# One decoder layer with PEER experts on one core: evacuation of the U products, order of the start and places of the last chunks changed

## The chip, the cores and the metric

The kernel runs on one NeuronCore of a Trainium2 chip. The metric is the device time of one execution in microseconds (us). Engines: PE (TensorE), ACT (ScalarE), DVE (VectorE), POOL (GpSimd), SP (SyncE, which issues DMAs here). One kernel launch computes the whole layer.

## The reference

For one sequence of 256 tokens with D = 2048 (T = 256 below) and one layer:

```
h = x + hybrid_mixer(rmsnorm(x, attn_norm), ...)          # NSA heads + sliding-window heads, out-projection
xn = rmsnorm(h, ffn_norm)
q = xn @ wq                                              # 8 heads, 2 halves of 128
s1, s2 = q[..., 0, :] @ subkeys[0].T, q[..., 1, :] @ subkeys[1].T
v1, i1 = top_k(s1, 16); v2, i2 = top_k(s2, 16)
sc, ci = top_k(v1[..., :, None] + v2[..., None, :], 16)  # 16 of the 256 sums
idx = i1[ci // 16] * 128 + i2[ci % 16]; gate = softmax(sc)
h = h + sum_k gate_k * gelu(xn . u[idx_k]) * v[idx_k]    # 16384 experts, U and V 16384 x 2048
out = rmsnorm(h, final_norm)
```

All of it is float32.

## The kernel before, in words

Matrix products that need float32 accuracy are made of three products of rounded parts: a matrix is split into a high part (`hi`, a rounded copy made by ACT, L114) and the rest (`lo`, raw minus hi, made by DVE, L115), and hi*Xhi + hi*Xlo + lo*Xhi are added in PSUM. `split` (L103) does that for the units of weights, which `load` (L93) brings in order through SP's queue; a unit is a [128, 1024] piece, 512 KB. `take` (L120) hands a unit to PE.

**Start.** `x` arrives in 8 pieces; `x_parts` (L153) makes its two halves (ACT L155, DVE L156). The V products (L244 to L246) run while `x` arrives; the squares of `x` (L249, ACT) are added by DVE (L258) and a matmul with ones sums them over partitions (L322, in `scale_rows`). `rms_scale` (L140) then makes the row of scales `rB` by ACT's square root (L146) and DVE's L147 to L151. The k and v projections (L173 to L175, `cols`) run meanwhile; the transposes of `rB` (L331), the gates (L340) and the compressed-key products (L304) stand among them in PE's order. Small tables (`posk`, `ohr`, `w2k` and so on) are issued on SP's queue as the code reaches them.

**Attention and out-projection** run to about 330 us, then the query projection of the PEER layer (`cols_wide`, L159) for 16 query columns i. Each i ends with `qs`: ACT copies one half of the product out of PSUM (L710), DVE adds the other (L711), PE multiplies with the sub-keys (L684), ACT scales into `ssb` (L687), and DVE takes the 16 best (`top16`, L672 to L678). Before the U products start, the scaled `x` is split once more into the two halves of X (ACT L717; L718 on DVE for even and POOL for odd blocks).

**U products.** 128 blocks of 128 experts. A block needs two units of U and either 16 pairs of a 512-column and a 256-column matmul (`cols_wide`: L165, L166; "wide") or 48 matmuls of 256 columns (`cols`: L173 to L175; "narrow", all three parts summed in one half of a PSUM bank). `u_end` (L656) empties the block's PSUM one block later: narrow by one Gelu of ACT (L662); wide by ACT's copy (L660), DVE's add (L661) and the Gelu. `product()` gives the next block one of a few PSUM buffers, so the block's first matmul (L165) waits until the older one is empty. The first `4 * LEAD` = 52 blocks run beside the routing:

```
            for n in range(4 * LEAD):
                u_block(n // 4, n % 4, n >= NARROW)
                settle()
                u_end(1)
                owed += BUDGET[n >= NARROW]
                while steps and owed > 0:
                    c, fn = steps.pop(0)
                    owed -= c
                    settle(1)
                    fn()
```

`steps` are the routing's pieces with estimated costs (candidate sums, top 16, picks by a one-hot comparison at L771 to L778 on DVE and POOL, index splits, `flip` with PE's transposes L793 to L795, `tok`), `BUDGET` how much of them is written per narrow and wide block. What is written is then ordered by a scheduler for each engine; `tc.high_priority()` moves a step ahead. Blocks 52 to 127 run beside the building of expert lists.

**V products and end.** 103 chunks of gathered V rows and weights, split like the rest (L1174, L1175; `a_parts`, `v_parts`), three products each (`v_products`, L1205) for two token halves t and four column quarters c. `finish` (L1233) adds a sum to the residual (L1236), squares it (L1238); `last_norm` (L1249) makes the scale r, scales (L1256, L1258) and issues the output DMAs (L1259).

Of the kernel before, what the change touches and what calls it, by code (L numbers as in the profile page):

```python
# [10 lines left out]
F32 = mybir.dt.float32  # L11
# [8 lines left out]
D = 2048  # L20
# [23 lines left out]
TG = 16  # L44
GSCALE = 2.0 ** 15
# [3 lines left out]
NARROW = 12  # L49
BUDGET = (2.75, 2.1)  # L50
# [4 lines left out]
def decoder_trunk(ctx, tc, xT, g1, g2, gf, w_cols, w_v, w_out, w_q, u, v, subk, posk, posv,  # L55
# [37 lines left out]
    def load():  # L93
# [6 lines left out]
        sp.dma_start(raw[:, :r * w], src)  # L100
        raws[i] = raw

    def split():  # L103
# [9 lines left out]
        with tc.high_priority():  # L113
            act.activation(hi[:, :n], raw[:, :n], AF.Copy)  # L114
            dve.tensor_tensor(lo[:, :n], raw[:, :n], f(hi[:, :n]), op=OP.subtract)  # L115
# [24 lines left out]
    def rms_scale(pool_, ps, dst):  # L140
# [5 lines left out]
        act.activation(s, ps, AF.Sqrt, bias=epst, scale=1.0 / D)  # L146
# [4 lines left out]
        dve.scalar_tensor_tensor(dst, s, 1.5, r, op0=OP.add, op1=OP.mult)  # L151

    def x_parts(db, src, g):  # L153

        act.activation(X[:, db, 0:T], src, AF.Copy, scale=g[:, db:db + 1])  # L155
        dve.scalar_tensor_tensor(X[:, db, T:], src, g[:, db:db + 1], f(X[:, db, 0:T]),  # L156
                                 op0=OP.mult, op1=OP.subtract)

# [27 lines left out]
    with ExitStack() as mx:  # L186
# [19 lines left out]
        sp.dma_start(g1t, g1)  # L206
# [26 lines left out]
        for k in range(8):  # L233
            if k + RAW < 8:
                load_x(k + RAW)
            for i in range(2):
                x_parts(2 * k + i, xt[:, 2 * k + i, :], g1t)
# [12 lines left out]
        sp.dma_start(relt[0:32, :], rel)  # L250
        sp.dma_start(ohrt, ohr)
        sp.dma_start(ohrbt, ohrb)
        sp.dma_start(pkv["k"], posk)
        sp.dma_start(pkv["v"], posv)
# [4 lines left out]
        sp.dma_start(g2t, g2)  # L259
        sp.dma_start(subkt, subk)  # L260
        sp.dma_start(w2kt, w2k)
        sp.dma_start(w2vt, w2v)
        sp.dma_start(sinkt, bass.AP(tensor=sinks.tensor, offset=sinks.offset, ap=[[0, 128], [1, 16]]))
# [47 lines left out]
        def tables():  # L311
            sp.dma_start(w1t["v"], w1v)
# [7 lines left out]
        def scale_rows():  # L320
            pss = ps1.tile([128, T], F32, name="tp", bufs=2)
            pe.matmul(pss, ones, ssum[:, 0], start=True, stop=True)  # L322
            sp.dma_start(w1t["k"], w1k)
# [270 lines left out]

        dve.tensor_scalar(nsink, sinkt, -1.0, None, op0=OP.mult)
# [36 lines left out]
    with ExitStack() as p3:  # L632
# [23 lines left out]
        def u_end(keep=0):  # L656
            while len(HU) > keep:
                ps, h, wide = HU.pop(0)
                if wide:
                    act.activation(h, ps[:, 1], AF.Copy)  # L660
                    dve.tensor_tensor(h, ps[:, 0], h, op=OP.add)  # L661
                act.activation(h, h if wide else ps[:, 0], AF.Gelu_apprx_tanh)  # L662

        with ExitStack() as pr:
# [34 lines left out]
            for i in range(1, 16):  # L699
# [10 lines left out]
                act.activation(qs, ps[:, 1], AF.Copy)  # L710
                dve.tensor_tensor(qs, ps[:, 0], qs, op=OP.add)  # L711
# [3 lines left out]
            with tc.high_priority():  # L715
# [707 lines left out]
```

## Time and profile before

| what | us |
|---|---|
| median of 3 runs (lowest, highest) | 1613.42 (1611.53, 1614.13) |
| the profiled execution | 1614.29 |
| its span, first to last instruction | 1612.5 |
| PE busy in it | 1586.9 (98%) |
| DVE busy | 1232.0 (76%) |
| ACT busy | 951.1 (59%) |
| POOL busy | 376.4 (23%) |

The profiled execution is 0.87 us above the median, and 1.8 us of it lie outside the span. PE's busy share says how little it idles, not that each of its matmuls runs at full speed: the granted clock in the windows says that. A wait names the instruction that released the waiting one.

### The profile page before, as it was taken

How to read it: one execution, taken by the hardware profiler on the slowest of the kernel's cores; microseconds unless marked ns; L12 is line 12 of the kernel's file. 1: busy time of each engine (PE TensorE's matmuls, PEld its weight loads, DVE VectorE, ACT ScalarE, POOL GpSimd, SP SyncE). 2: the span in 40 equal slices, each digit the busy share in tenths (PEclk: the TensorE clock that was granted, in tenths of full speed). 3: DMA queues.
4: the chain of work that ended last, by engine and by line, in shares of the span. 5: the costliest groups of instructions: out<-in, count | busy, mean ns of one | idle time of the engine just before them, and what ended most of it. 6: DMA issues, size and time to landing. Idle time of an engine off the chain costs nothing.

```text
span 1612.5 us, 26938 instructions
## 1 busy us (share of the span) xinstructions
PE 1586.9 (98%) x9870; PEld 1370.9 (85%) x9870; DVE 1232.0 (76%) x2291; ACT 951.1 (59%) x1638; POOL 376.4 (23%) x354
## 2 busy tenths in 40 slices
PE   9999999999999999999999999999999999999996
PEld 8998888888898888888888888888887878788885
DVE  7698886779999987678668767665555788888886
ACT  6587775554643666667545444444445676777675
POOL 0010111143133410000000000000003666677770
PEclk9999999999999999999999999999999999999998
DMA  9544434555455576666999976688765879899992
GB/s 318 172 156 128 135 121 146 182 175 178 158 173 167 160 252 218 216 207 238 299 334 356 307 247 206 209 265 276 234 221 210 317 280 340 297 365 346 347 348 81
DMA packets 135224, 378.33 MB, mean 235 GB/s; under 512 B 11976, under 2 KB 67372, under 8 KB 119212
## 3 DMA queue, kind: packets, MB, share of 16 engines
q1 hardware_dynamic: 115596, 257.51, 48.6%
q0 software_dynamic: 18912, 117.98, 19.5%
q8 instruction: 79, 1.29, 0.3%
q10 hardware_dynamic: 576, 1.05, 0.2%
q14 instruction: 61, 0.50, 0.1%
HBM read 341.05 MB, written 35.44 MB: 233 GB/s over the span
## 4 chain that ended last, share of the span: by engine, by line
PE 91%; DVE 5%; ACT 1%; issue 1%; POOL 1%; DMA 1%; SPq 0%; DVEq 0%; POOLq 0%; ACTq 0%
PE mm L165 29%; PE mm L166 15%; PE pv L1210 6%; PE pv L1212 6%; PE pv L1211 6%; PE mm L573 3%; PE mm L173 3%; PE mm L175 3%; PE mm L174 3%; PE mm L1210 2%; PE mm L1212 2%; PE mm L1211 2%; PE tp L837 2%; PE mm L574 2%; DVE lo L115 1%
## 5 line engine op out<-in xcount | busy, mean ns | idle before, releaser
L165 PE MATMUL mm<-X,hi 128*128 128x512 f32 x2096 | 751.7, 399 | 6.0 <-DVE hg L661 6.0
L114 ACT ACTIVATE hi<-raw 128x1024 fp32r<-128x1024 f32 (+1 forms) x370 | 389.8, 1055 | 401.1 <-issue 185.3
L115 DVE TENSOR_TENSOR lo<-raw,hi 128x1024 fp32r<-128x1024 f32 (+1 forms) x370 | 458.8, 1242 | 205.4 <-ACT hi L114 202.7
L166 PE MATMUL mm<-X,lo 128*128 128x256 f32 x2096 | 592.0, 283 | 0.4 <-DVE lo L115 0.4
L165 PEld LDWEIGHTS mm<-X,hi 128*128 128x128 f32 x2096 | 394.8, 188 | 97.8 <-DVE hg L661 6.9
L166 PEld LDWEIGHTS mm<-X,lo 128*128 128x128 f32 x2096 | 394.7, 188 | 1.7 <-DVE lo L115 1.4
L1175 DVE TENSOR_TENSOR lo<-hg,hi 128x1024 fp32r<-128x1024 f32 x210 | 256.1, 1224 | 68.8 <-ACT hi L1174 64.0
L1174 ACT ACTIVATE hi<-hg 128x1024 fp32r<-128x1024 f32 x210 | 221.6, 1058 | 95.7 <-PE pv L1212 76.9
L1084 POOL DMA_INDIRECT hg<-in_v_dram,idxV x103 | 129.3, 1256 | 451.4 <-ACT hg L662 296.8
L173 PE MATMUL mm<-X,hi 128*128 128x256 f32 x544 | 157.8, 290 | 0.0
L175 PE MATMUL mm<-X,lo 128*128 128x256 f32 x544 | 154.0, 283 | 0.2 <-DVE lo L115 0.2
L174 PE MATMUL mm<-X,hi 128*128 128x256 f32 x544 | 153.9, 283 | 0.0
L1092 POOL DMA_INDIRECT ar<-At,idxA x103 | 116.7, 1133 | 96.7 <-issue 60.4
L1211 PE MATMUL pv<-lo,ah 128*128 128x512 f32 x396 | 136.7, 395 | 0.0
L1212 PE MATMUL pv<-hi,al 128*128 128x512 f32 x396 | 135.3, 396 | 0.0
L1210 PE MATMUL pv<-hi,ah 128*128 128x512 f32 x396 | 123.0, 397 | 1.8 <-ACT ah L1162 1.6
L173 PEld LDWEIGHTS mm<-X,hi 128*128 128x128 f32 x544 | 103.7, 191 | 4.3 <-issue 3.9
L175 PEld LDWEIGHTS mm<-X,lo 128*128 128x128 f32 x544 | 103.3, 190 | 1.4 <-DVE lo L115 1.1
L174 PEld LDWEIGHTS mm<-X,hi 128*128 128x128 f32 x544 | 103.4, 190 | 0.5 <-issue 0.4
L1210 PEld LDWEIGHTS pv<-hi,ah 128*128 128x128 f32 x396 | 74.4, 188 | 21.8 <-ACT ah L1162 2.3
L1212 PEld LDWEIGHTS pv<-hi,al 128*128 128x128 f32 x396 | 74.4, 188 | 18.2
L1211 PEld LDWEIGHTS pv<-lo,ah 128*128 128x128 f32 x396 | 74.4, 188 | 17.5
(299 smaller groups left out, 2109.8 us busy)
## 6 DMA issues: line engine op xcount, KB each, us to landing
raw<-in_u_dram SPq DMA_DIRECT2D x256, 512.0 KB, 4.7
raw<-in_w_cols_dram SPq DMA_DIRECT2D x42, 512.0 KB, 3.5
raw<-in_w_out_dram SPq DMA_DIRECT2D x32, 512.0 KB, 4.7
raw<-in_w_q_dram SPq DMA_DIRECT2D x32, 512.0 KB, 4.2
gs<-stg SPq DMA_DIRECT2D x16, 1024.0 KB, 4.8
gt<-gs SPq DMA_DIRECT2D x16, 1024.0 KB, 9.0
At<-a SPq DMA_DIRECT2D x31, 512.0 KB, 6.7
tb<-bd SPq DMA_DIRECT2D x16, 256.0 KB, 3.6
```

Source lines behind the costliest of these rows:

```text
L114: act.activation(hi[:, :n], raw[:, :n], AF.Copy)
L115: dve.tensor_tensor(lo[:, :n], raw[:, :n], f(hi[:, :n]), op=OP.subtract)
L165: pe.matmul(ps.rearrange("p a t -> p (a t)"), hi[:, i, :], X[:, db], start=db == 0, stop=False)
L166: pe.matmul(ps[:, 0], lo[:, i, :], X[:, db, 0:T], start=False, stop=db == DB - 1)
L173: pe.matmul(ps, hi[:, i, :], X[:, db, 0:T], start=db == 0, stop=False)
L174: pe.matmul(ps, hi[:, i, :], X[:, db, T:], start=False, stop=False)
L175: pe.matmul(ps, lo[:, i, :], X[:, db, 0:T], start=False, stop=db == DB - 1)
L1174: act.activation(hi, r_, AF.Copy)
L1175: st2["lo"] = dve.tensor_tensor(lo, r_, f(hi), op=OP.subtract)
L1210: pe.matmul(ps, ah[:, tl], hi[:, cl], start=first, stop=False)
L1211: pe.matmul(ps, ah[:, tl], lo[:, cl], start=False, stop=False)
L1212: pe.matmul(ps, al[:, tl], hi[:, cl], start=False, stop=last)
```

## The change

1. `NARROW` goes from 12 to 26 and the narrow `BUDGET` from 2.75 to 2.5: 14 blocks become narrow.
2. `u_end` gets a `room`: for the wide blocks 26 to 51 ACT copies both halves out of PSUM, and DVE adds two SBUF tiles.
3. The `qs` copy and add get high priority; the second split of X is issued behind the last `qs` add (`issue_after` holds instructions of the same engine, here the even blocks' L718 on DVE).
4. The start: the norm weights `g1` go through ACT's queue, the first split is cut in two pieces, the squares come later, and the small tables wait in SP's order for the weights loaded so far.
5. The end: the last chunk is split early into places of its own (pool `lp`, once `part` is closed), the last 48 products stand in strict order of t and c, the last quarter is finished in two pieces of 256, and the first half's outputs leave during the second half's products.

```diff
-NARROW = 12
-BUDGET = (2.75, 2.1)
+EARLY = 4
+NARROW = 26
+BUDGET = (2.5, 2.1)
...
-        def u_end(keep=0):
+        def u_end(keep=0, room=None):
             while len(HU) > keep:
                 ps, h, wide = HU.pop(0)
                 if wide:
                     act.activation(h, ps[:, 1], AF.Copy)
-                    dve.tensor_tensor(h, ps[:, 0], h, op=OP.add)
+                    one = ps[:, 0]
+                    if room:
+                        one = room.tile([128, T], F32, name="half", bufs=2)
+                        act.activation(one, ps[:, 0], AF.Copy)
+                    dve.tensor_tensor(h, one, h, op=OP.add)
                 act.activation(h, h if wide else ps[:, 0], AF.Gelu_apprx_tanh)
...
-                act.activation(qs, ps[:, 1], AF.Copy)
-                dve.tensor_tensor(qs, ps[:, 0], qs, op=OP.add)
+                with tc.high_priority():
+                    act.activation(qs, ps[:, 1], AF.Copy)
+                    summed = dve.tensor_tensor(qs, ps[:, 0], qs, op=OP.add)
...
-            with tc.high_priority():
+            with tc.high_priority(), tc.issue_after(summed.ins):
                 for db in range(DB):
...
-        sp.dma_start(g1t, g1)
+        act.dma_start(g1t, g1)
...
+            if k == 0:
+                with tc.issue_after(xa.ins):
+                    split(2)
...
-            if k % 2 == 1:
-                c = k // 2
-                act.activation(sqs[:, 4 * c:4 * c + 4], xt[:, 4 * c:4 * c + 4, :], AF.Square)
+            if k in (3, 7):
+                with tc.issue_after(pos["high"].ins):
+                    for c in (0,) if k == 3 else (1, 2, 3):
+                        act.activation(sqs[:, 4 * c:4 * c + 4], xt[:, 4 * c:4 * c + 4, :], AF.Square)
...
+        with tc.issue_after(pos["loaded"].ins):
+            sp.dma_start(pkv["k"], posk)
...
+                if i == len(SEQ) - EARLY:
...
+                    pp.close()
+                    lp = pv_.enter_context(tc.tile_pool(name="lp", bufs=1))
+                    m = SEQ[-1]
+                    with tc.issue_after(st2["lo"].ins):
+                        held[m] = v_parts(m, [[lp.tile([128, HALF], F32R, name=f"last{x_}{h}") for x_ in range(2)] for h in range(2)])
+                        pa[m] = a_parts(m, [lp.tile([128, T], F32R, name=f"lastA{x_}") for x_ in range(2)])
...
+            done = None
             for t in range(2):
                 for c in range(4):
                     for n in SEQ[-2:]:
-                        v_products(n, t, c, *pa[n], held[n])
-                    finish(t, c)
-                last_norm(t)
+                        with tc.issue_after(done.ins) if done else ExitStack():
+                            done = v_products(n, t, c, *pa[n], held[n])
+                    added = finish(t, c)
+                    with tc.issue_after(added.ins):
+                        if c % 2 == 0:
+                            ahead(t, c)
+                        for c_ in ((), (), (1, 0), (3,))[c] if t else ():
+                            put_out(0, c_)
+                root = last_norm(t)
```

Three places show how the order moves. The first is PE's order where the query products end (L165, L166; L170, L171 in the change) and the U products begin (L173 to L175; L178 to L180); the key products are L684 (L705). Before:

```order
L166 MATMUL mm<-X,lo 128x256
L684 MATMUL tp<-subkt,qs 128x128 x2
L173 MATMUL mm<-X,hi 128x256
L174 MATMUL mm<-X,hi 128x256
L175 MATMUL mm<-X,lo 128x256
...
L175 MATMUL mm<-X,lo 128x256
L684 MATMUL tp<-subkt,qs 128x128 x2
L173 MATMUL mm<-X,hi 128x256
L174 MATMUL mm<-X,hi 128x256
```

In the change:

```order
L171 MATMUL mm<-X,lo 128x256
L705 MATMUL tp<-subkt,qs 128x128 x2
L178 MATMUL mm<-X,hi 128x256
L705 MATMUL tp<-subkt,qs 128x128 x2
L178 MATMUL mm<-X,hi 128x256
L179 MATMUL mm<-X,hi 128x256
L180 MATMUL mm<-X,lo 128x256
```

The key product of the last query, which stood behind the 48 matmuls of the first block, stands behind the first of them.

The second is DVE's order at the same place. Here `qs` is the sum of the last query (L711; L733), `X` the second split (L718; L740), `lo` the units (L115; L118), and the others are steps of the 16 best. Before:

```order
L115 TENSOR_TENSOR lo<-raw,hi 128x1024
L676 MATCH_REPLACE mr<-VI,ssb 128x128
L718 TENSOR_TENSOR X<-hg,X 128x256 x3
L677 MAX VI<-mr 128x8
L718 TENSOR_TENSOR X<-hg,X 128x256
L678 MAX_INDEX VI<-VI,mr 128x8
L115 TENSOR_TENSOR lo<-raw,hi 128x1024
L673 MAX VI<-ssb 128x8 x2
L711 TENSOR_TENSOR qs<-mm,qs 128x256
L674 MAX_INDEX VI<-VI,ssb 128x8
```

In the change:

```order
L118 TENSOR_TENSOR lo<-raw,hi 128x1024
L699 MAX_INDEX VI<-VI,mr 128x8
L118 TENSOR_TENSOR lo<-raw,hi 128x1024
L733 TENSOR_TENSOR qs<-mm,qs 128x256
L740 TENSOR_TENSOR X<-hg,X 128x256 x8
L694 MAX VI<-ssb 128x8 x4
L695 MAX_INDEX VI<-VI,ssb 128x8
```

All eight of DVE's X steps stood ahead of the last `qs` add (four are in the piece above); now all eight stand in a row behind it.

The third is PE's order in the projections of the start: the sum of the squares (L322; L334), the bias tables (L315; L327) and the transposes of `rB` (L331; L344) among the triples of the k and v products. Before:

```order
L175 MATMUL mm<-X,lo 128x256
L322 MATMUL tp<-early,ones 128x256
L173 MATMUL mm<-X,hi 128x256
L174 MATMUL mm<-X,hi 128x256
L315 MATMUL tp<-early,relt 16x384
L175 MATMUL mm<-X,lo 128x256
...
L175 MATMUL mm<-X,lo 128x256
L315 MATMUL tp<-early,relt 16x384
L173 MATMUL mm<-X,hi 128x256
...
L175 MATMUL mm<-X,lo 128x256
L331 MATMUL tp<-ident,rB 128x128 x2
L173 MATMUL mm<-X,hi 128x256
```

In the change:

```order
L179 MATMUL mm<-X,hi 128x256
L334 MATMUL tp<-early,ones 128x256
L327 MATMUL tp<-early,relt 16x384
L180 MATMUL mm<-X,lo 128x256
L178 MATMUL mm<-X,hi 128x256
...
L180 MATMUL mm<-X,lo 128x256
L327 MATMUL tp<-early,relt 16x384
L344 MATMUL tp<-ident,rB 128x128 x2
L178 MATMUL mm<-X,hi 128x256
```

The sum of squares stood 75 places ahead of the transposes; now 19 places lie between them.

## Rows read from the trace of the kernel before

**Rows 1.** Page: busy us, share of the span and count of each engine.

```profile
PE 1586.9 (98%) x9870; PEld 1370.9 (85%) x9870; DVE 1232.0 (76%) x2291; ACT 951.1 (59%) x1638; POOL 376.4 (23%) x354
```

**Rows 2.** Windows of core 0; columns as in the first line.

```profile
core 0: us, PE busy (x) PEld busy (x) DVE busy (x) ACT busy (x) POOL busy (x), PEclk, DMA share, GB/s
...
428.60:500.00 71.40, 70.07 (x588) 69.33 (x587) 68.89 (x189) 36.34 (x51) 29.53 (x28) 1.00 0.51 163
500.00:520.00 20.00, 17.31 (x88) 14.35 (x87) 19.42 (x75) 7.03 (x15) 5.17 (x11) 0.91 0.57 185
...
540.00:560.00 20.00, 18.73 (x127) 16.08 (x126) 18.72 (x26) 9.48 (x15) 11.88 (x8) 1.00 0.52 164
...
1599.50:1612.50 13.00, 0.00 (x0) 0.00 (x0) 6.10 (x20) 5.12 (x13) 0.00 (x0) 0.65 0.45 166
```

**Rows 3.** Waits of PE, 420 to 660 us.

```profile
PE mm L165 <- DVE hg L661: 3.9, 3, 2.3
PE tp L684 <- DVE qs L711: 1.1, 1, 1.1
PE mm L166 <- DVE lo L115: 0.4, 1, 0.4
```

**Rows 4.** Timeline of PE, 500 to 519 us: start, duration, instruction.

```profile
514.16 0.51 PE L165 MATMUL mm<-X,hi 128*128 128x512 f32 x1 [2.26 <-DVE hg L661]
...
517.15 0.63 PE L165 MATMUL mm<-X,hi 128*128 128x512 f32 x1
```

**Rows 5.** Timeline of DVE, 488 to 516 us.

```profile
494.17 2.00 DVE L115 TENSOR_TENSOR lo<-raw,hi 128x1024 fp32r<-128x1024 f32 x1
...
498.00 1.22 DVE L115 TENSOR_TENSOR lo<-raw,hi 128x1024 fp32r<-128x1024 f32 x1
```

**Rows 6.** Timeline of POOL, 484 to 504 us.

```profile
493.91 3.09 POOL L774 TENSOR_TENSOR hit<-hit,pay 128x400 f32<-128x400 f32 x2 [1.23 <-DVE hit L771]
```

**Rows 7.** Lines by form: group, count, busy us, mean ns; ACT, then DVE.

```profile
L660 ACT ACTIVATE hg<-mm 128x256 f32<-128x256 f32 x116 | 42.6, 367 | 25.3 <-PE mm L166 25.3
...
L661 DVE TENSOR_TENSOR hg<-mm,hg 128x256 f32<-128x256 f32 x116 | 48.3, 416 | 7.4 <-ACT hg L660 7.3
L1164 DVE TENSOR_TENSOR al<-ar,ah 128x256 fp32r<-128x256 f32 x13 | 5.4, 418 | 0.0
```

**Rows 8.** Timeline of ACT, 424 to 437 us.

```profile
429.57 1.06 ACT L114 ACTIVATE hi<-raw 128x1024 fp32r<-128x1024 f32 x1
```

**Rows 9.** Timeline of PE, 424 to 437 us.

```profile
424.02 0.40 PE L165 MATMUL mm<-X,hi 128*128 128x512 f32 x1
...
424.37 0.40 PE L165 MATMUL mm<-X,hi 128*128 128x512 f32 x1
...
435.67 0.71 PE L684 MATMUL tp<-subkt,qs 128*128 128x128 f32 x4 [1.09 <-DVE qs L711]
```

**Rows 10.** Timeline of PE, 29 to 42 us.

```profile
30.64 0.59 PE L322 MATMUL tp<-early,ones 128*128 128x256 f32 x2
...
41.44 0.38 PE L331 MATMUL tp<-ident,rB 128*128 128x128 f32 x2
```

**Rows 11.** Timeline of ACT, 18 to 45 us.

```profile
33.09 1.28 ACT L146 ACT_TABLE_LOAD   x1
```

**Rows 12.** Timeline of DVE, 18 to 45 us.

```profile
35.23 1.74 DVE L148 RECIPROCAL row<-row 128x256 f32<-128x256 f32 x1
...
39.88 0.42 DVE L151 SCALAR_TENSOR_TENSOR rB<-row 128x256 f32<-128x256 f32 x1
```

**Rows 13.** Windows at the start; columns as in rows 2.

```profile
50.50:57.30 6.80, 6.80 (x34) 6.80 (x33) 4.09 (x11) 4.88 (x11) 0.22 (x1) 0.50 0.44 152
```

**Rows 14.** Timeline of DVE, 1588 to 1613 us.

```profile
1599.54 0.68 DVE L1236 TENSOR_TENSOR acc<-mm,acc 128x512 f32<-128x512 f32 x1
...
1602.32 1.42 DVE L1256 SCALAR_TENSOR_TENSOR raw<-acc,r,gft 128x512 f32<-128x512 f32 x2
...
1604.49 1.41 DVE L1256 SCALAR_TENSOR_TENSOR raw<-acc,r,gft 128x512 f32<-128x512 f32 x2
```

More of the change, by code (lines that the diff above doesn't have):

```diff
@@ L113, in split @@
         with tc.high_priority():
[L114 to L115 removed]
+            for k in range(pieces):
+                p_ = slice(n * k // pieces, n * (k + 1) // pieces)
+                pos["high"] = act.activation(hi[:, p_], raw[:, p_], AF.Copy)
+                dve.tensor_tensor(lo[:, p_], raw[:, p_], f(hi[:, p_]), op=OP.subtract)
         parts[i] = (hi[:, :n].rearrange("p (a b) -> p a b", a=r),
@@ L235, in decoder_trunk @@
                 load_x(k + RAW)
-            for i in range(2):
-                x_parts(2 * k + i, xt[:, 2 * k + i, :], g1t)
+            with tc.high_priority() if k == 0 else ExitStack():
+                for i in range(2):
+                    xa = x_parts(2 * k + i, xt[:, 2 * k + i, :], g1t)
+            if k == 0:
+                with tc.issue_after(xa.ins):
+                    split(2)
             hi, lo = take(1)
@@ L1144, in decoder_trunk, with a_parts @@
         assert not todo and not owing and weighed == 31
-        def a_parts(n):
+        def a_parts(n, room=None):
             ar = AR.pop(n) if n >= 0 else AL[4 + n]
-            ah = kp.tile([128, T], F32R, name="ah", bufs=2)
-            al = kp.tile([128, T], F32R, name="al", bufs=2)
+            ah, al = room or [kp.tile([128, T], F32R, name=x_, bufs=2) for x_ in ("ah", "al")]
             order = ORDERS[phase[n]]
@@ L1165, in a_parts, with v_parts @@
             return ah, al
-        def v_parts(n):
+        def v_parts(n, room=None):
             raw = VR.pop(n)
@@ L1170, in v_parts @@
             for h in range(2):
-                hi = stream.tile([128, HALF], F32R, name="hi")
-                lo = stream.tile([128, HALF], F32R, name="lo")
+                hi, lo = room[h] if room else [stream.tile([128, HALF], F32R, name=x_) for x_ in ("hi", "lo")]
                 r_ = raw[:, HALF * h:HALF * h + HALF]
@@ L1211, in v_products @@
                 pe.matmul(ps, ah[:, tl], lo[:, cl], start=False, stop=False)
-                pe.matmul(ps, al[:, tl], hi[:, cl], start=False, stop=last)
-            part = vp.tile([128, 2, D], F32, name="part")
+                return pe.matmul(ps, al[:, tl], hi[:, cl], start=False, stop=last)
+            pp = pv_.enter_context(ExitStack())
+            part = pp.enter_context(tc.tile_pool(name="pp", bufs=1)).tile([128, 2, D], F32, name="part")
             owed = []
@@ L1233, in finish @@
             def finish(t, c):
-                s = acc[t][:, 512 * c:512 * c + 512]
-                dve.tensor_tensor(s, sums[t, c], s, op=OP.add)
-                sc = vp.tile([128, 512], F32, name="sc", bufs=2)
-                act.activation(sc, s, AF.Square, accum_out=sq4[:, t, c:c + 1])
+                w = 256 if t and c == 3 else 512
+                for k in range(512 // w):
+                    s = acc[t][:, 512 * c + w * k:512 * c + w * k + w]
+                    added = dve.tensor_tensor(s, sums[t, c][:, w * k:w * k + w], s, op=OP.add)
+                    sc = vp.tile([128, 512], F32, name="sc")[:, 0:w]
+                    act.activation(sc, s, AF.Square, accum_out=sq4[:, t, c + k:c + k + 1])
                 if t == c == 0:
@@ L1297, in decoder_trunk @@
                     for n in SEQ[-2:]:
-                        v_products(n, t, c, *pa[n], held[n])
-                    finish(t, c)
-                last_norm(t)
+                        with tc.issue_after(done.ins) if done else ExitStack():
[7 more added lines that the diff above has]
+                root = last_norm(t)
+            with tc.issue_after(root.ins):
+                put_out(0, 2)
+            for c in (1, 0, 3, 2):
+                put_out(1, c)
         pm.close()
```

72 lines of the change are left out of this document (40 added, 32 removed).

## The prediction

> **What bounds the kernel now.** I read the busy shares first, then windows by stage, then the waits of PE, and last the timelines at the places that the change touches. PE is busy 1586.9 us of the span of 1612.5 [rows 1], so 25.6 us is all that lies outside its matmuls; 13.0 of these are the tail behind the last matmul [rows 2]. No part of the change removes a matmul: it can only fill PE's gaps, shorten the tail, or move the stretches in which PE's granted clock is low.
>
> The routing stage is where PE's gaps and a second busy engine meet. From 428.6 to 500 DVE is busy 68.89 of 71.40 us, from 500 to 520 it is 19.42 of 20, from 540 to 560 it is 18.72 of 20, while ACT is half idle in all three [rows 2]. The waits of PE between 420 and 660 us add to 5.4 us in three lines: 3.9 for a block's first matmul, released by DVE's add L661 which empties the old PSUM buffer, 1.1 for the last query's `qs`, 0.4 for a `lo` [rows 3]. The longest, 2.26 us, ends at 514.16, and behind it matmuls take 0.63 us [rows 4] where 0.40 is usual [rows 9]: that is the level of 1.2 GHz. The mean clock of that window, 0.91 [rows 2], makes 0.09 x 20 / 0.5 = 3.6 us at this level; the loss is 3.6 x (1 - 0.40/0.63) = 1.3 us. So the routing stage holds 3.9 + 0.4 + 1.3 = 5.6 us to be won, without the boundary to the queries.
>
> **The change, part by part.**
>
> *Narrow blocks (12 to 26) and the room.* For PE a narrow block costs what a wide one does: 588 matmuls in 70.07 us are 0.119 each [rows 2], so 48 make 5.7; a pair of the wide form takes 424.37 - 424.02 = 0.35 [rows 9], so 16 make 5.6. That is 14 x 0.1 at most, and I count nothing. DVE loses 14 adds of 0.416, 5.8 us; ACT loses 14 copies of 0.367, 5.1, and gains 26 second copies of about as much, 9.5 [rows 7]. ACT's 4.4 net are hidden: it is busy 7.03 and 9.48 of 20 [rows 2]. In blocks 26 to 51 DVE's add no longer holds PSUM, so the 3.9 can go, and with the 2.26 the slow stretch of 1.3 behind it. If ACT's idle time were gone, its two copies would hold PSUM longer than its one does now.
> The add itself now reads two SBUF tiles. The nearest rows price that: 0.418 with both inputs in SBUF against 0.416 [rows 7]; I add nothing.
>
> *What is late next: `lo`.* Where DVE no longer holds PSUM it still makes every `lo`, and the waits for `lo` are already there [rows 3]. In DVE's new order all eight X steps (8 x 0.42 by the like-sized row [rows 7] = 3.3 us) and steps of the 16 best stand in one run ahead of the next `lo`, where they were spread before. DVE has only 71.40 - 68.89 = 2.5 us of idle time in that stretch [rows 2] to take this up, and the narrow blocks are the ones with the most routing work. I estimate that PE waits 1.8 us more there than before, nearer to 3.3 - 2.5 = 0.8 than to the upper end; the ends are 0 (the run is absorbed) and 6 (the 3.3 in full, and about as much again where later routing steps are pulled ahead).
>
> *The boundary from queries to U.* The key product of the last query stood behind block 0, and now stands behind one matmul of it. What it needs hardly moves. ACT makes the `hi` of 429.57, until 430.63 [rows 8], then one X step of about 0.4 and the `qs` copy; DVE makes the `lo` of that `hi`, 1.22 [rows 5], until 431.9, and then the add of about 0.4: 432.2. PE is there at about 428.8, so it waits 3.4, where it now waits 1.1 [rows 3, 9]: 2.3 lost. Bounds: 0, if DVE takes the add ahead of that `lo`, to 3.6, if a slow stretch like the one behind the 2.26 follows (1.3 more).
> Routing with the boundary: 5.6 - 1.8 - 2.3 = **1.5 won**; ends 5.6 won and 4.0 lost.
>
> *The start.* The earlier first split and the weights that no longer queue behind small tables let PE run ahead; I estimate up to 2.4 us by the end of the V products. But the sum of squares (L322) now stands only 19 places ahead of the transposes of `rB` (L331), about 2.5 us of PE work, instead of 75. Between them lie, in series, the table load of 1.28 [rows 11], the reciprocal of 1.74 and links of about 0.42 like the last [rows 12]: 1.28 + 1.74 + 8 x 0.42 = 6.4 us. Today these two stand at 30.64 and 41.44 [rows 10], so the chain is covered; in the change PE stands still for some 3 us and passes L331 at about 41.4 again. The lead is given back there. The slow stretch behind it, 34 matmuls in 6.8 us at a clock of 0.50 [rows 13], would take 34 x 0.119 = 4.1 at full clock, so 2.7 hang on whether it stays. I take 0.5 won, for waits ahead of it that go; ends 3.2 won (stretch gone too) and 2.7 lost (a second one behind the new stall).
>
> *The end.* Products and their number stay. Now DVE finishes its last add at 1600.9 behind half-column work, serves the first half's scaling from 1602.32 for 1.42 us, and starts the second half's last scaling at 1604.49, ending 1605.9 [rows 14], 6.4 behind the last matmul at 1599.5. In the change the first half is out before that, the last add is half as long (0.68 to about 0.4), and the square is too; scaling in the same 1.41 ends about 4.5 behind the last matmul: **1.9 won**, with ends 0.5 (only the shorter add and square) and 2.5. The DMAs behind it are the same.
>
> Sum: 1614.3 - 1.5 - 0.5 - 1.9 = 1610.4 for an execution like the profiled one (1614.29). That one lies 0.87 above the median of the runs, so against the median of 1613.42 I predict **1609.5 us**.
>
> **The rivals.** About 0.2% (3.2 us) is what a measurement of this kernel can tell from no change: faster means below 1610.2, slower above 1616.6.
>
> *More is won.* The `lo`s stay ahead and the boundary costs no more than today: 5.6 in the routing; the slow stretch of the start goes: 3.2; the end 1.9. That is 10.7, 1602.7 us. For it: the waits of rows 3 name L661 and almost nothing else, and DVE loses 5.8 us. Against it: DVE's busy share, and the run of X steps.
>
> *The waits change their name only.* What PE waited for at L661 it waits for at `lo`, since DVE is the engine behind both and has no less to do in the first 26 blocks; or ACT's copies stand behind a `hi` and PSUM comes free no earlier. Routing with boundary at 0, start at 0, end 1.9: 1611.5; with the boundary's 2.3 in full 1613.8; I say 1612.
>
> *Slower: DVE becomes the bound of blocks 0 to 51.* The wait at the boundary costs 2.3 and, being longer than 2.26, a slow stretch of 1.3; `lo` costs the 6 of its upper end. And where POOL works at its side, DVE's instructions with two SBUF inputs get longer: a `lo` took 2.00 beside POOL's L774 and 1.22 without it [rows 5, 6]. The 26 adds now are of that kind: 26 x 0.78, for POOL's share of 5.17 to 11.88 in 20 us [rows 2] some 8.7 us, of which DVE's idle time of 500 to 600 us hides about 6. With 2.7 left: 2.3 + 1.3 + 6 + 2.7 - 5.6 - 0.5 - 1.9 = +4.3, 1617.7 us. It decides where these terms come to more than 11.2 of their 12.3.
> The Trainium skill says so in "SBUF — State Buffer", section "Who interferes with whom": a VectorE instruction with two SBUF inputs contends with a GpSimd instruction that reads SBUF, and the one that comes second is blocked until the other is through. The two durations of `lo` agree with it; whether L661, with one input in PSUM, is spared today, no row here shows by itself. By this rule alone the change would give up to 2.7 us back; by the 0.418 of the like row, nothing.
>
> **How the numbers follow.** Forecast 0.50, by itself 1606.5 to 1611.5; more won 0.18; a change of names only 0.20; slower 0.12. The range takes the forecast and most of the first two rivals and the near part of the last: 1603.0 to 1615.5. Faster by over 0.2%: 0.18 + 0.40 of the forecast's 0.50 = 0.58. Slower: 0.12. The rest, 0.30, is within 0.2%.
>
> **What the profile of the changed kernel would show.** Right: no wait of PE for L661's successor between 500 and 600 us and no clock below 1.00 there; a wait of about 3 us at the second key product near 429; a stall of about 3 us ahead of the transposes of `rB` near 40; and the last output issued some 4.5 us behind the last matmul. Wrong: waits for `lo` in the first 26 blocks of more than 4 us in all, adds L661 much over 0.42 us, or a second stretch at 0.50 at the start. If PE passes the transposes of `rB` before 40 us, the start's term is wrong; if the boundary shows no wait, that of the boundary.

## The result and the profile after

The change makes the kernel slower: a median of 1622.95 us (1620.41 to 1626.87) against 1613.42; ratio 1.0067, 95% interval 1.0054 to 1.0079. The forecast was 1609.5 with a range up to 1615.5, so both the sign and the range were wrong. The profiled execution took 1625.63 us, its span is 1623.8. The top of its page:

```profile
span 1623.8 us, 27400 instructions
...
PE 1589.6 (98%) x10094; PEld 1386.1 (85%) x10094; DVE 1229.2 (76%) x2278; ACT 955.9 (59%) x1653; POOL 380.2 (23%) x355
```

PE's busy time is 2.7 us longer than before [rows 1], while the span is 11.3 longer. The waits of PE over the whole run (us in total, times, longest) begin with three that were not there before, or far smaller:

```profile
PE tp L705 <- DVE qs L733: 3.7, 1, 3.7
PE tp L859 <- DVE o L849: 3.5, 1, 3.5
PE tp L344 <- DVE rB L154: 3.1, 1, 3.1
PE mm L170 <- DVE hg L682: 1.6, 1, 1.6
...
PE mm L180 <- DVE lo L118: 1.2, 1, 1.2
```

L705 is the key product (L684 before), L859 the one-hot token product (L837), L344 the transposes of `rB` (L331), L170 the first matmul of a wide block (L165), and L180 a matmul of a narrow one. The waits for DVE's add did shrink: in 420 to 660 us, where they were 3.9 [rows 3], there is none left. The clock tells the rest. Windows of the same run, columns as in rows 2:

```profile
36.00:50.00 14.00, 10.88 (x60) 9.19 (x59) 11.72 (x28) 6.08 (x11) 0.00 (x0) 0.76 0.79 285
428.60:440.00 11.40, 7.71 (x48) 7.33 (x47) 9.52 (x37) 5.60 (x16) 5.49 (x6) 0.85 0.35 116
590.00:610.00 20.00, 16.51 (x134) 15.21 (x133) 18.38 (x27) 8.89 (x10) 3.12 (x2) 0.83 0.69 238
840.00:855.00 15.00, 12.56 (x56) 10.35 (x55) 10.45 (x17) 7.20 (x12) 0.00 (x0) 0.77 0.96 305
```

The third number from the end (0.76, 0.85, 0.83, 0.77) is the granted clock: up to the last matmul there are four stretches at 1.2 GHz where the kernel before had two. All four begin during or right behind a wait of the list above. The timeline of PE shows it for the third; the matmul of two tokens takes 0.39 and 0.41 where its like took 0.28 four us earlier:

```profile
595.81 0.28 PE L859 MATMUL tp<-o,hot 128*128 128x128 f16 x2
...
599.63 0.39 PE L859 MATMUL tp<-o,hot 128*128 128x128 f16 x2 [3.49 <-DVE o L849]
...
599.93 0.41 PE L859 MATMUL tp<-o,hot 128*128 128x128 f16 x2
```

The window of that stretch alone has the half clock throughout:

```profile
598.40:605.23 6.83, 5.60 (x33) 5.15 (x34) 6.80 (x11) 2.15 (x2) 0.00 (x0) 0.50 1.00 342
```

PE worked 5.60 us of it, so at most 2.8 us were lost behind the wait. The fourth stretch is another matter: the wait of 1.6 us at it stood in the kernel before too, and had none there (timelines of PE, the change, then before):

```profile
844.79 0.79 PE L170 MATMUL mm<-X,hi 128*128 128x512 f32 x1 [1.62 <-DVE hg L682]
```

```profile
850.51 0.50 PE L165 MATMUL mm<-X,hi 128*128 128x512 f32 x1 [1.54 <-DVE hg L661]
```

None of the twelve profiles of the experiments has a slow stretch there either. This execution is 2.7 us above the median of the change, about what the prediction estimated for a stretch of that length.

At the end the outputs wait for a chain of DVE and ACT (timelines of DVE and of POOL):

```profile
1606.80 0.69 DVE L1259 TENSOR_TENSOR acc<-mm,acc 128x512 f32<-128x512 f32 x1 [0.22 <-PE mm L1232]
...
1607.60 1.83 DVE L1284 SCALAR_TENSOR_TENSOR raw<-acc,r,gft 128x512 f32<-128x512 f32 x1
1609.35 0.74 DVE L1259 TENSOR_TENSOR acc<-mm,acc 128x256 f32<-128x256 f32 x2
1610.02 0.74 DVE L1284 SCALAR_TENSOR_TENSOR raw<-acc,r,gft 128x512 f32<-128x512 f32 x1
...
1612.24 1.41 DVE L1284 SCALAR_TENSOR_TENSOR raw<-acc,r,gft 128x512 f32<-128x512 f32 x2
```

```profile
1607.58 1.30 POOL L1273 TENSOR_TENSOR raw<-acc,gft 128x512 f32<-128x512 f32 x1 [24.11 <-DVE r L154]
```

The scaling L1284 takes 1.83 us at 1607.60 and 0.74 at 1610.02. What differs is POOL's product at its side (the run without that product is below). The last adds, whose matmuls were through at 1608.15, wait for it until 1609.35. The first half's outputs do not leave during the second half's products: their first is issued at 1609.46, 1.3 us behind the last matmul. And the span does not end with the outputs: the last is issued near 1614, and the last instructions stand at 1623.8. The lines of the program's closing instructions (L1419 before, L1468 after; shortest, middle and longest in ns, then first and last start), of the kernel before and of the change:

```profile
L1419 POOLq DRAIN  x3: 40/107/8308, 1582.2 to 1612.2; - x3
```

```profile
L1468 POOLq DRAIN  x3: 40/107/8309, 1614.7 to 1623.5; - x3
...
L1468 ACTq DRAIN  x2: 8/37/66, 1618.8 to 1623.2; - x2
```

Both kernels have a closing DRAIN of 8.31 us on POOL. Before, it began at 1582.2 and was over at 1590.5, beside the V products. In the change it begins at 1614.7 and is over at 1623.0, and the span ends 0.8 behind it. The other engines have begun their closing steps by 1618.8 (ACT is the last) and make the rest of them near 1623.2, behind that DRAIN. So the end of the span is POOL's, and the 1.1 us by which the scaling is longer are hidden in it.

To compare runs I cut each profile at three places: the start of the first query product (the first L165 of before), the end of the last U product, and the end of the last matmul.

| profiled run | first query product | from it to the last U product | V products | behind the last matmul | span |
|---|---|---|---|---|---|
| before | 336.9 | 889.9 | 372.6 | 13.0 | 1612.5 |
| after | 338.8 | 897.0 | 372.4 | 15.7 | 1623.8 |
| difference | +1.8 | +7.0 | -0.2 | +2.6 | +11.3 |

### The profile page after: what moved, and what is told of

It reads as the page before. It is cut to its first block, busy times and chain, and to the rows that moved or that the text cites. A ratio compares the mean times of both kernels' runs of the same rounds, so it can differ in the third digit from the quotient of the medians.

```text
span 1623.8 us, 27400 instructions
## 1 busy us (share of the span) xinstructions
PE 1589.6 (98%) x10094; PEld 1386.1 (85%) x10094; DVE 1229.2 (76%) x2278; ACT 955.9 (59%) x1653; POOL 380.2 (23%) x355
## 4 chain that ended last, share of the span: by engine, by line
PE 65%; DVE 5%; issue 1%; DMA 1%; ACT 1%; POOL 0%; ACTq 0%; SPq 0%; POOLq 0%
PE mm L170 23%; PE mm L171 12%; PE pv L1230 6%; PE pv L1231 6%; PE pv L1232 6%; PE mm L1230 2%; PE mm L1231 2%; DVE lo L118 2%; PE mm L1232 2%; PE tp L859 2%; PE mm L180 1%; PE mm L178 1%; PE mm L179 1%; PE pc L863 1%; DVE hit L793 1%
## 5 line engine op out<-in xcount | busy, mean ns | idle before, releaser
L170 PE MATMUL mm<-X,hi 128*128 128x512 f32 x1872 | 672.0, 400 | 1.6 <-DVE hg L682 1.6
L117 ACT ACTIVATE hi<-raw 128x1024 fp32r<-128x1024 f32 (+2 forms) x371 | 389.9, 1053 | 427.3 <-issue 196.1
L118 DVE TENSOR_TENSOR lo<-raw,hi 128x1024 fp32r<-128x1024 f32 (+2 forms) x371 | 457.5, 1235 | 218.9 <-ACT hi L117 215.0
L171 PE MATMUL mm<-X,lo 128*128 128x256 f32 x1872 | 529.9, 283 | 0.4 <-DVE lo L118 0.4
L170 PEld LDWEIGHTS mm<-X,hi 128*128 128x128 f32 x1872 | 354.1, 189 | 83.6 <-DVE hg L682 1.8
L171 PEld LDWEIGHTS mm<-X,lo 128*128 128x128 f32 x1872 | 353.8, 189 | 0.9 <-DVE lo L118 0.7
L178 PE MATMUL mm<-X,hi 128*128 128x256 f32 x768 | 221.3, 288 | 0.0
L180 PE MATMUL mm<-X,lo 128*128 128x256 f32 x768 | 217.2, 283 | 1.3 <-DVE lo L118 1.2
L179 PE MATMUL mm<-X,hi 128*128 128x256 f32 x768 | 216.9, 283 | 0.0
L178 PEld LDWEIGHTS mm<-X,hi 128*128 128x128 f32 x768 | 146.3, 190 | 3.5 <-issue 3.2
L180 PEld LDWEIGHTS mm<-X,lo 128*128 128x128 f32 x768 | 145.9, 190 | 2.8 <-DVE lo L118 1.9
L179 PEld LDWEIGHTS mm<-X,hi 128*128 128x128 f32 x768 | 146.1, 190 | 0.4 <-issue 0.4
L1232 PEld LDWEIGHTS pv<-hi,al 128*128 128x128 f32 x390 | 73.3, 188 | 17.4
```

The costliest lines, as they stand in the source:

```text
L117: pos["high"] = act.activation(hi[:, p_], raw[:, p_], AF.Copy)
L118: dve.tensor_tensor(lo[:, p_], raw[:, p_], f(hi[:, p_]), op=OP.subtract)
L170: pe.matmul(ps.rearrange("p a t -> p (a t)"), hi[:, i, :], X[:, db], start=db == 0, stop=False)
L171: pe.matmul(ps[:, 0], lo[:, i, :], X[:, db, 0:T], start=False, stop=db == DB - 1)
L178: pe.matmul(ps, hi[:, i, :], X[:, db, 0:T], start=db == 0, stop=False)
L179: pe.matmul(ps, hi[:, i, :], X[:, db, T:], start=False, stop=False)
```

## The experiments

The kernel before ran beside each of the three groups and the last run, with medians of 1612.02, 1612.73, 1612.12 and 1612.01 us. I therefore compare by ratios to it; 0.001 is 1.6 us.

| run | edit | median us | ratio (95%) | first query product | to last U | behind last matmul |
|---|---|---|---|---|---|---|
| e1_no_pool_end | after, no POOL product | 1617.48 | 1.0028 (1.0014 to 1.0041) | 338.0 | 894.2 | 11.1 |
| e2_squares_early | after, squares as before | 1615.26 | 1.0017 (1.0001 to 1.0033) | 335.6 | 893.9 | 15.5 |
| e3_narrow12 | after, 12 narrow blocks | 1623.77 | 1.0067 (1.0042 to 1.0091) | 338.1 | 896.6 | 15.2 |
| e4_queries_as_before | after, query order as before | 1616.19 | 1.0023 (1.0009 to 1.0037) | 337.2 | 889.3 | 15.5 |
| c1_start_and_end | before + start + end | 1608.20 | 0.9966 (0.9954 to 0.9978) | 332.4 | 890.2 | 11.4 |
| c2_without_query_order | c1 + narrow + room | 1607.31 | 0.9967 (0.9952 to 0.9981) | 333.3 | 888.3 | 11.6 |
| c4_narrow_no_room | c1 + narrow | 1607.75 | 0.9967 (0.9952 to 0.9981) | 336.1 | 887.2 | 11.7 |
| c5_room_narrow12 | c1 + room | 1609.99 | 0.9987 (0.9976 to 0.9999) | 333.1 | 891.3 | 11.1 |
| c7_issue_after_alone | c2 + issue_after | 1610.87 | 0.9991 (0.9980 to 1.0002) | 333.2 | 892.3 | 11.7 |
| c8_budget_2p3 | c2, narrow budget 2.3 | 1600.02 | 0.9927 (0.9907 to 0.9947) | 332.3 | 882.1 | 11.5 |
| c9_budget_no_room | c8 without the room | 1601.24 | 0.9936 (0.9919 to 0.9952) | 333.1 | 881.6 | 11.3 |
| pd_pool_end_alone | before + POOL product | 1616.28 | 1.0021 (1.0006 to 1.0036) | 335.4 | 888.7 | 17.4 |

In the table "start" is the changed start with the squares where they were, "end" the changed end without POOL's product, and "narrow" the 26 narrow blocks with their budget of 2.5.

**The end: POOL's late product.**

```diff
-                eng = pool if t and c == 2 else dve
-                eng.tensor_tensor(scaled[t, c], ...)
+                dve.tensor_tensor(scaled[t, c], ...)
```

> The changed kernel, with the last-quarter product of the second half given to DVE instead of POOL. Theory (the end is POOL's): in both kernels POOL closes with a DRAIN of 8.31 us; before, it began at 1582.2 and lay beside V products; in the change it begins at 1614.66, because POOL's product of 1607.58 waits for the first half's scale, and the span ends when it ends. Without that product the DRAIN starts near 1580 again, DVE's scaling of 1607.60 takes 0.7 instead of 1.83, and the span ends about 10.5 us behind the last matmul instead of 15.9: 5 us faster than the changed kernel. Rival (POOL's product is help): DVE takes 0.69 more in the chain, the end moves by -0.5 to +0.7 us.

Measured: 1.0067 falls to 1.0028, 6 us. In the profile the span ends 11.1 us behind the last matmul instead of 15.7; these 4.6 are the end's. POOL's DRAIN is back beside the V products, and the scaling is short again (closing line, then DVE's timeline of this run):

```profile
L1467 POOLq DRAIN  x3: 40/107/8308, 1587.6 to 1615.5; - x3
```

```profile
1604.70 0.74 DVE L1283 SCALAR_TENSOR_TENSOR raw<-acc,r,gft 128x512 f32<-128x512 f32 x1
1605.36 0.75 DVE L1259 TENSOR_TENSOR acc<-mm,acc 128x256 f32<-128x256 f32 x2
```

The rival, that POOL's product is help, is out. DVE's last scaling ends 5.0 us behind the last matmul (1604.71), in the change 5.5:

```profile
1608.31 1.42 DVE L1283 SCALAR_TENSOR_TENSOR raw<-acc,r,gft 128x512 f32<-128x512 f32 x2
```

The converse is the kernel before with that one product moved to POOL:

```diff
-                    dve.tensor_tensor(o, s, gft[...], op=OP.mult)
+                    (pool if t and c == 2 else dve).tensor_tensor(o, s, gft[...], op=OP.mult)
```

> The kernel before with one edit: the scaling product of the last half's third quarter is made by POOL instead of DVE. Theory (POOL's closing DRAIN of 8.31 us counts once POOL has late work): POOL's product runs at about 1600.5, its closing steps last 7 us as in the changed kernel, the DRAIN begins near 1608.5 and the span ends 0.8 behind it, near 1617.7: 5 us slower than before. Rival (the DRAIN only fills idle time): the end stays with the output DMAs, within 1 us of before.

Measured: 1.0021 (1.0006 to 1.0036), 3.4 us slower, and in the profile 17.4 us behind the last matmul instead of 13.0: 4.4 us.

```profile
1597.49 1.29 POOL L1247 TENSOR_TENSOR raw<-acc,gft 128x512 f32<-128x512 f32 x1 [25.66 <-DVE tot L1250]
```

```profile
L1419 POOLq DRAIN  x3: 40/107/8308, 1604.9 to 1613.8; - x3
```

The product ends at 1598.8, the DRAIN begins at 1604.9, ends at 1613.2, and the span at 1614.0. From the start of POOL's product to the end of the DRAIN it is 15.7 us here and 15.4 in the change. One product of 1.3 us on an otherwise finished engine costs about three times its length.

**The start: late squares.**

```diff
-            if k in (3, 7):
-                with tc.issue_after(pos["high"].ins):
-                    for c in (0,) if k == 3 else (1, 2, 3):
-                        act.activation(sqs[...], xt[...], AF.Square)
+            if k % 2 == 1:
+                c = k // 2
+                act.activation(sqs[...], xt[...], AF.Square)
```

> The changed kernel, with the squares of x where they were (one step of four blocks at every second piece of x), so that the sum of squares stands 57 places ahead of the transposes of rB instead of 19. Theory (the late sum of squares costs the start): the 3.1 us wait for rB goes, the transposes are passed near 39.5, the second split stage starts 2 us earlier than in the kernel before, and the whole is 2.5 to 3 us faster than the changed kernel. Rival (the lead is lost anyway, to the gates or to weights that are not there): the wait goes, but the compressed-key products start within 0.5 us of where they do in the changed kernel, less than 1 us faster.

Measured: the transposes of `rB` stand at 40.29 without a wait, 42.80 in the change with 3.1 us of wait (timelines of PE, the change first), 41.44 before [rows 10]; the query products begin 3.1 us earlier than in the change.

```profile
42.80 0.69 PE L344 MATMUL tp<-ident,rB 128*128 128x128 f32 x2 [3.12 <-DVE rB L154]
```

```profile
40.29 0.38 PE L342 MATMUL tp<-ident,rB 128*128 128x128 f32 x2
```

The theory holds for the start. The whole gained 8 us by ratio, more than the 3 expected; in the profile 3.1 lie in the start and 3.1 in the U products, where the slow stretch near 844 us is missing, as in every profile but that of the change. That part I can't put down to the edit.

**The queries' end.**

```diff
-                with tc.high_priority():
-                    act.activation(qs, ps[:, 1], AF.Copy)
-                    summed = dve.tensor_tensor(qs, ps[:, 0], qs, op=OP.add)
+                act.activation(qs, ps[:, 1], AF.Copy)
+                dve.tensor_tensor(qs, ps[:, 0], qs, op=OP.add)
...
-            with tc.high_priority(), tc.issue_after(summed.ins):
+            with tc.high_priority():
```

> The changed kernel without the high priority of the last query sum and without the order behind it: the key product of the last query stands behind block 0 again, the X steps ahead of it. Theory (the boundary costs what its wait shows): the 3.7 us wait becomes about 1.1 and the 3.4 us stretch at half clock (1.6 us) goes: 4 us faster than the changed kernel. Rival (DVE's backlog only moves): PE waits for lo in the first blocks instead; within 1 us.

Measured: 1.0023, 7 us faster than the change. The wait is 1.1 again, no slow stretch follows, and the stretch from the queries to the last U product falls from 897.0 to 889.3. These 7.7 us are not the boundary's alone: 2.6 are the shorter wait, the slow stretch of 3.4 us behind it lost at most 1.7, and the stretch near 844 us is missing here too. The waits of PE from 420 to 700 us in this run:

```profile
PE tp L858 <- DVE o L848: 4.2, 1, 4.2
PE tp L705 <- DVE qs L732: 1.1, 1, 1.1
```

Which of the two pieces does it? The second alone, put into a kernel without the other losses:

```diff
-                dve.tensor_tensor(qs, ps[:, 0], qs, op=OP.add)
+                summed = dve.tensor_tensor(qs, ps[:, 0], qs, op=OP.add)
...
-            with tc.high_priority():
+            with tc.high_priority(), tc.issue_after(summed.ins):
```

> The kernel of the run without query order, with one piece of it put back: the X steps are issued behind the last query sum (issue_after), without the high priority of the sum. PE's key product of the last query then stands behind the first matmul of block 0 again. Theory (that place on PE is the loss): a wait of 3.7 us there with a stretch at half clock behind it, 5 us slower than the kernel without query order. Rival (the high priority is the loss, it moves the 16 best behind): no long wait, within 1.5 us.

Measured: 0.9991 against 0.9967, 4 us slower, with the wait and the slow stretch (timeline of PE):

```profile
429.40 1.22 PE L703 MATMUL tp<-subkt,qs 128*128 128x128 f32 x4 [4.07 <-DVE qs L730]
```

The same product in c2:

```profile
432.03 0.71 PE L703 MATMUL tp<-subkt,qs 128*128 128x128 f32 x4 [1.08 <-DVE qs L730]
```

The window of c7:

```profile
425.00:440.00 15.00, 10.93 (x81) 10.73 (x81) 13.03 (x63) 6.97 (x14) 4.48 (x6) 0.89 0.29 93
```

So `issue_after`, which orders only DVE's X steps, moved PE's key product from behind block 0 to behind its first matmul, and that place is the loss. The sum itself did come earlier, as the X steps no longer stand ahead of it: its product starts 2.6 us sooner than in c2. But PE reaches the product 5.6 us sooner (429.40 - 4.07 = 425.33 against 432.03 - 1.08 = 430.95), so it waits 3.0 us longer. The high priority alone was not run.

**The routing: narrow blocks, room, budget.**

```diff
-NARROW = 26
-BUDGET = (2.5, 2.1)
+NARROW = 12
+BUDGET = (2.75, 2.1)
```

> The changed kernel with NARROW 12 and BUDGET (2.75, 2.1) as before; room, order of the queries, start and end as changed. Theory (the narrow blocks bring the token steps too close together): the wait of 3.5 us for the one-hot product at 599.6 and the stretch at half clock behind it, 2.8 us, go; the room keeps PSUM waits at 0 from 500 to 660; 5 to 7 us faster than the changed kernel. Rival (DVE is short by as much in any order): the wait comes back at another place, for lo or hg, with its stretch; within 2 us of the changed kernel.

Measured: 1.0067, no change. The wait at the one-hot product's matmul stays, 4.5 us instead of 3.5 (the profile names ACT's `hi` as what came last before it). The rival has the time right, but the wait is not at `lo` or at the add, as it said.

```profile
PE tp L859 <- ACT hi L117: 4.5, 1, 4.5
```

Then the parts on a base without the three losses. First the start and the end alone (this kernel has `NARROW` 12, `BUDGET` (2.75, 2.1), no room, and the queries as before):

> The kernel before with the changed start (squares left where they were) and the changed end (no product on POOL); routing and queries as before. Theory (the parts add up, each by its own stage): U products begin 1.3 us earlier than before, as in the run with early squares, they last as long as before, and the span ends 11.3 instead of 13.3 us behind the last matmul, as in the run without POOL: 3.3 us faster than the kernel before. Rival (the routing's waits take the lead back, as its DVE work is no earlier): 2 us faster at most, from the end alone.

Measured: 0.9966, 5.5 us faster, more than the theory's 3.3. The start has 4.5 us less, some 3 of which lie where the slow stretch of rows 13 was, which this run does not have; the end has 1.6 less; the U products are as long as before. PE still waits for DVE's add, 3.9 us from 420 to 700. Now with 26 narrow blocks and the room; with the narrow blocks only; with the room only:

> All of the change but three pieces: squares where they were, no product on POOL at the end, query sum and X steps as before. 26 narrow blocks and the room stay. Theory (parts add up): start -1.3, U products -0.6 as in the run with the queries as before, end -2.0: 3.9 us faster than the kernel before, 13 faster than the changed kernel. Rival (the wait for the one-hot product, 4.2 us and its slow stretch, grows by what the start gains): 1 to 2.5 us faster than the kernel before.

> The kernel of the run without query order, with the room taken away as well: DVE's add reads PSUM again in blocks 26 to 51; 26 narrow blocks stay. Theory (the room is worth nothing, since PE's long wait is for the one-hot product now): within 1.5 us of that kernel, PE waits for hg under 1.5 us between 560 and 780. Rival (the room carries the gain): the waits for hg come back, 4 us and more in all, 3 us slower than that kernel.

> The kernel of the run without query order with NARROW 12 and BUDGET (2.75, 2.1): room alone. Theory (room and narrow blocks each only turn the wait for PSUM into the wait for the one-hot product): a wait of 3.5 to 4.5 us for it remains near 600, waits for hg under 2 us from 500 to 660, time within 2 us of the kernel with neither (1608.2). Rival (narrow blocks made that wait, the room alone is the gain): no wait over 1 us at the one-hot product, 4 us faster than the kernel with neither.

The edits are `NARROW` and `BUDGET` as above, and for the room

```diff
-                u_end(1, rt)
+                u_end(1)
...
-            u_end(0, rt)
+            u_end()
```

Measured: 0.9967, 0.9967 and 0.9987 against 0.9966 with neither. 26 narrow blocks change nothing in the time, with or without the room, and the room with 12 is 3 us slower. c2 is 5.3 us faster than the kernel before, where its theory had 3.9, but c1 without the blocks and the room is as fast. The theory of c4 holds; that of c5 holds for the wait, while the time is above its 2 us. In all three the waits for the add between 420 and 700 us are gone and a wait for the one-hot product of 3.7, 3.7 and 5.0 us has come, as here with both:

```profile
PE tp L856 <- DVE o L846: 3.7, 1, 3.7
```

The last idea was the place of that wait. PE's order has two token groups in a row behind block 25, and DVE is late with the second. A smaller budget writes the routing steps later; the groups near block 25 then stand apart, and the first pair in a row stands behind block 29:

```diff
-BUDGET = (2.5, 2.1)
+BUDGET = (2.3, 2.1)
```

> The kernel of the run without query order with a narrow budget of 2.3 instead of 2.5: the routing steps are written about two blocks later, and the two token groups that stood together behind block 25 stand apart there. Theory (the one-hot wait comes from two groups in one block while DVE is behind): the wait falls from 3.7 to under 1 us and its slow stretch goes; 3 to 5 us faster than that kernel, about 1603.5. Rival (DVE's backlog decides, not the grouping): the wait appears at the next pair, within 1.5 us.

Measured: 0.9927 (0.9907 to 0.9947), 1600.02 us, 6.4 faster by ratio than with 2.5, above the 3 to 5 of the theory. Between 420 and 700 us the wait for the one-hot product is 0.8 in two pieces and the waits for the add are gone, and up to the last matmul no window has a clock below 1.00:

```profile
PE tp L856 <- DVE o L846: 0.8, 2, 0.5
```

```profile
20.00:60.00 40.00, 39.61 (x308) 37.72 (x308) 31.95 (x58) 23.33 (x36) 0.22 (x1) 1.00 0.80 261
428.00:440.00 12.00, 10.92 (x92) 10.70 (x91) 11.90 (x47) 5.69 (x9) 0.02 (x1) 1.00 0.49 163
500.00:700.00 200.00, 199.12 (x1602) 184.34 (x1602) 158.51 (x248) 119.36 (x174) 28.69 (x19) 1.00 0.63 210
700.00:1590.00 890.00, 884.38 (x4932) 743.44 (x4930) 655.46 (x822) 521.55 (x763) 248.40 (x209) 1.00 0.80 280
```

The rival, the same wait at the next pair, is out: the pair behind block 29 waits 0.5 us at most. But two things move together with this number, the place of the pair and the work that DVE has been given by then. No run separates them.

Is it the room that pays, now that nothing hides it?

> The kernel of the run with a narrow budget of 2.3, with the room taken away: DVE's add reads PSUM again in blocks 26 to 51. Theory (the room is what keeps PSUM free once the token wait is gone): waits for hg of 3 to 5 us between 575 and 700 with a slow stretch behind the longest, 3 to 6 us slower than with the room. Rival (with 26 narrow blocks and later routing steps DVE's add is on time anyway): waits for hg under 1.5 us, within 1.5 us of 1600.0.

Measured: 1601.24 us, 0.9936; the intervals overlap widely. The waits for the add come back with 0.9 us:

```profile
PE mm L170 <- DVE hg L680: 0.9, 1, 0.9
```

So no gain of the room can be told from none: 1.2 us by the medians, 0.1 by the spans of the two profiles (1598.4 and 1598.3). The gain is 26 narrow blocks with the smaller budget. A smaller budget with 12 narrow blocks was not tried.

## Why the prediction was wrong

**The end: the step that failed is "the first half is out before that ... 1.9 won".** It followed DVE and ACT only and left POOL's new product out. With that product the closing steps and the DRAIN of 8.31 us lie at the end, 15.7 us behind the last matmul instead of 13.0; this is shown by taking the product away (e1) and by adding it to the kernel before (pd). What the step said of DVE and ACT came in part. Even without POOL the first half is not out early (in e1 its first output is issued at 1605.47, 0.8 us behind the last matmul), and the last scaling ends 5.0 us behind the last matmul, not 4.5: 1.4 of the 1.9 were won there. That the span of e1 ends 2.0 us nearer to the last matmul than before is close to 1.9 by luck; 0.6 of it came behind the scaling, where the prediction expected nothing.

POOL's product also blocked DVE's scaling beside it, 1.83 for 0.74 us, but that is hidden behind POOL's closing steps. The Trainium skill's "SBUF — State Buffer", section "Who interferes with whom", has it: a VectorE instruction with two SBUF inputs and a GpSimd instruction that reads SBUF exclude each other, and the later one waits. The trace agrees: 1607.58 + 1.30 and 1607.60 + 1.83 begin together and only POOL's runs at its usual length (1.29 in pd). I cited the rule for the 26 adds with room, L682 in the change. They took 0.42 us each, but they run between 612 and 788 us, where POOL is busy for 0.5 us in all, so this run does not test the rule on them; the rival had taken POOL's share from 500 to 560 us.

**The boundary: right mechanism, the better case taken.** The wait was given as 3.4 us and is 3.7. The slow stretch behind it was only in the upper bound (3.6 lost); it came, and c7 puts the price at 4 us (e4's 7 by ratio hold more than the boundary). The one wait of this size before, the 2.26 of rows 4, had such a stretch behind it. In the fourteen profiles kept here PE has 21 waits of 2.2 to 5.1 us, and each has a slow stretch of 3.4 or 6.8 us that begins within 1.4 us of its end; of the waits of 1.0 to 1.8 us only the one at 844.79 has.

**The routing: the steps that failed are "in blocks 26 to 51 DVE's add no longer holds PSUM, so the 3.9 can go" and "what is late next: `lo`".** The 3.9 were not in blocks 26 to 51. They are the waits that end at 514.16, 553.04 and 580.46, at blocks 14, 20 and 24; the second of them in the timeline of PE of the kernel before:

```profile
553.04 0.50 PE L165 MATMUL mm<-X,hi 128*128 128x512 f32 x1 [1.27 <-DVE hg L661]
```

The change makes those blocks narrow, and that took the waits away. From 590 to 780 us, where blocks 26 to 51 ran, PE had no wait for the add that the room could save; c4 agrees, and c9 but for 0.9 us. (In c5 the room took them away, as it covers the wide blocks from 12 on there.) DVE is indeed what is late next, and the 3.9 us went as forecast. But PE does not pay at `lo`, where I put 1.8 us more than before (1.2 measured in all, against the 0.4 of rows 3 and a 0.2 that they leave out); it pays in one piece at the one-hot product behind block 25, 3.5 us and a slow stretch that loses at most 2.8. I had not looked at who else waits for DVE there: that product has no wait for DVE in the trace of before, probably because PE came later, held up by the add. The rival "the waits change their name only" was nearest for the routing, though it too looked at `lo`: c1, c2 and c4 show another name and the same time, c5 3 us more. I gave it 0.20. c8 shows its limit: with the smaller budget the wait and its slow stretch are all but gone.

**The start: the wait right, the sum wrong.** 3.1 us at the transposes were forecast as some 3, but they are passed at 42.8, not 41.4. The prediction's own terms had said so: 6.4 - 2.5 = 3.9 us of wait against a lead of at most 2.4 cannot end at 41.4 again. Measured, the lead is 1.8 (the wait begins at 39.7) and the wait 3.1. The slow stretch moved there, from 50.4 to 42.0, instead of going. Started from +0.5 won, the query products begin 1.8 later; 0.95 of that lies in the out-projection, which the change doesn't touch (see below), so the term is 0.9 lost.

Together: start -0.9 instead of +0.5, U products and boundary -7.0 instead of +1.5, end -2.6 instead of +1.9, out-projection -0.95. In the -7.0 is the stretch near 844 us, some 2.7 us by the prediction's price for one of that length, which I can't put down to the change. The slower rival had the sign and DVE as its cause, but not the places: its 6 us at `lo` and its lengthened adds did not occur; blocks 0 to 25 show 1.2 us of waits for `lo`. Most signs that the prediction gave for being right did come: no wait for the add between 500 and 600 us, the wait at the second key product, the stall ahead of `rB`. The full clock there did not, and none of the signs looked at the one-hot product or at what stands behind the outputs.

## What to carry to other kernels

Before giving an idle engine a late product, look at what that engine does between its last instruction and the end of the program: an engine that finished early may be hiding its closing work. When a wait for a busy engine is removed, list every consumer of that engine behind that place, those without a wait today first, because they may be on time only thanks to the wait. Look also at which blocks the waits stand in before giving other blocks more room. And a wait of 2 to 5 us on TensorE is to be priced with the slow stretch behind it: writing the late engine's work later, here by one number of a budget, gained 6.4 us (c8 against c2), as much as the good parts of the change gained without it (5.3 in c2).

## What the runs showed that I had not expected

- POOL's closing DRAIN takes 8.31 us in all fourteen profiles kept here, whenever it begins (1569.8 in the fastest kernel, 1614.7 in the change).
- Where no long wait stands at them, the slow stretches come and go between executions of the same code. The start of c2 and of c4 is the same; the window from 48 to 56 us has a clock of 1.00 in the one and 0.57 in the other:

```profile
48.00:56.00 8.00, 8.00 (x72) 8.00 (x71) 4.07 (x12) 6.02 (x13) 0.22 (x1) 1.00 0.71 186
```

```profile
48.00:56.00 8.00, 8.00 (x45) 8.00 (x44) 4.05 (x11) 4.89 (x11) 0.22 (x1) 0.57 0.62 173
```

  The single runs of the kernel before fit that: 1609.08 us at a mean clock of 0.996, 1616.56 and 1619.50 at 0.993. So a difference of some 3 us between two profiles can be one stretch; the medians and the stage table have to be read together, and e2's surplus stays open for that reason.
- The out-projection, untouched by any edit, takes 103.1 us from its first matmul to its last in some profiles (before, c1, c8) and 104.1 in others (after, c2, c7, pd), spread over many matmuls. What decides it was not tried.
